# Two MLPs by seven products each level: another order of the first seven products, and operand sums made in halves

## The chip, the cores and the metric

The kernel runs on one core of a Trainium2 chip as one program. The metric is the device time of a run in microseconds. The engines have their own instruction queues and run each queue in order: PE (TensorE, the matrix products), DVE (VectorE), ACT (ScalarE), POOL (GpSimd), and SP, which here only issues DMAs. Engines wait for each other through semaphores.

## The reference, cut to what matters

Two decoder layers over 1024 positions of width 1024, all in float32. Each layer is an attention mixer followed by an MLP, both between norms:

```
x = x + rms_norm(mixer(rms_norm(x)))
x = x + rms_norm(square(relu(rms_norm(x) @ w1)) @ w2)      # w1: 1024x4096, w2: 4096x1024
```

Only the MLP line is touched by the change, in both layers.

## The kernel before, in words

**Products.** The class `Mlp` (L1052) cuts the 4096 inner columns into four groups of 1024. For each group it forms "up", a 1024x1024x1024 product of a weight block with the activations, takes the squared relu, and forms "down", the product with the block of w2, which is added into `acc`. Each such product is not done as eight products of 512x512x512 blocks but as seven, with sums and differences of blocks as operands (a Winograd scheme). The seven have the numbers 1 to 7; `left` (L1101) makes the weight operand and `right` (L1150) the activation operand of a number. In the first group of "up" they are, with weight blocks w00, w01, w10, w11 and activation blocks x00, x10 (first 512 positions) and x01, x11 (last 512):

```
1: w00 * x00          2: w01 * x10          6: s2 * t2        5: (w00 + s2) * (x01 - x00)
7: (w00 - w10) * t3   3: (w01 - s2) * x11   4: w11 * (x10 - t2)
with s2 = w11 - (w00 - w10),  t3 = x11 - x01,  t2 = t3 + x00
```

x11 is the fourth activation block, the one that is complete last; product 3 takes it as it is, unsummed. The sums are written in place where they can be: w01 is overwritten by w01 - s2.

**Precision.** `parts` (L1078) turns every operand of 128x2048 into a rounded part `hi` (ACT, L1083) and a remainder `lo` (L1084, on POOL for weights, on DVE for first-group activations), both in two halves of 1024 columns. One number then is 48 matmuls (L1262): four output quarters j, four inner blocks q, and hi*hi, hi*lo, lo*hi for each. A row names them as out<-moving,stationary.

**Banks.** `product` (L1243) puts the output quarters of a number into one of two sets of PSUM banks by the parity of its place: set A (three `psM` and one `psO`, 512 columns each) or set B (two `psS` pairs of 1024 columns). Numbers 1, 2 and 5 start a sum in their set and the others are accumulated onto what stands there. `evac` (L1268) brings the running sums out: a plain copy by ACT (L1291) when a quarter of the result is first written, and otherwise a DVE addition (L1293) followed by the squared relu (L1294). The old order is 1, 2, 6, 5, 7, 3, 4, with the sets A B A B A B A.

**Order.** `run` (L1313) goes through all 56 steps: `prep` of the next step (operands), `loads` (L1222: DMAs of weights, and, in the first group, stores of the activation operands to DRAM from which later groups read them back), `product`, `evac`. At step 0 it also calls `finish`, which transposes the last 128 positions into x01 and x11 (L369 on PE, copies on ACT L372). This is the order of priority: a scheduler then orders each engine's queue by it and by its own model of when operands are there. Only SP keeps the written order. `Mem` hands out SBUF pages in the order in which they were freed, so an operand can also wait for the last reader of its page.

The sums of operands are all made by one helper, `comb` (L1089), in one DVE instruction of 128x2048 (L1090).

Of the kernel before, what the change touches and what calls it, by code (L numbers as in the profile page):

```python
# [17 lines left out]
ALU = mybir.AluOpType  # L18
# [114 lines left out]
def hybrid_kernel(ctx: ExitStack, tc: tile.TileContext, x, pos, g_mix_pre, g_mix_post, g_ffn_pre, g_ffn_post,  # L133
# [918 lines left out]
    class Mlp:  # L1052
# [5 lines left out]
        UP, DOWN = (1, 2, 6, 5, 7, 3, 4), (1, 5, 6, 3, 7, 2, 4)  # L1058

        def __init__(self, layer):  # L1060
            self.layer = layer
            self.td = tc.dram_tile([7, P, 4096], F32, name=f"t_d{layer}")
            self.w1, self.w2, self.h, self.sums = {}, {}, {}, {}
            self.ready = {}
            self.tq = {}
            self.acc = [None] * 4
            self.steps = []
            for g in range(GROUPS):
                self.steps += [("up", g, n, i) for i, n in enumerate(self.UP)]
                self.steps += [("down", g, n, i) for i, n in enumerate(self.DOWN)]  # L1070
            self.bank = {}
# [17 lines left out]
        def comb(self, out, a, b, op, eng=None):  # L1089
            (eng or nc.vector).tensor_tensor(out, a, b, op=op)  # L1090
            return out
# [9 lines left out]
        def left(self, kind, g, n):  # L1101
# [5 lines left out]
            add, sub = ALU.add, ALU.subtract  # L1107
            if kind == "up":
# [41 lines left out]
        def right(self, kind, g, n):  # L1150
# [4 lines left out]
            if kind == "up":  # L1155
# [6 lines left out]
                elif n == 6:  # L1162
# [3 lines left out]
                    self.comb(t2, t3, r[0, 0], add)  # L1166
                    res = self.parts(t2, lo, True)
# [4 lines left out]
                elif n == 7:  # L1172
                    res = self.parts(r.pop("t3"), lo)
                elif n == 3:
                    res = self.parts(r.pop((1, 1)), lo)
                else:
                    self.comb(r["t2"], r[1, 0], r["t2"], sub)
                    free(r.pop((1, 0)))
                    res = self.parts(r.pop("t2"), lo)
# [63 lines left out]
        def product(self, s, js=range(4)):  # L1243
            kind, g, n, i = self.steps[s]
            (sh, sl), (th, tl) = self.ready[s]
            new = n == 1 or n == (2 if kind == "up" else 5) or n == (5 if kind == "up" else 2)
            if new and js[0] == 0:
                if s % 2:
                    b = [psS(), psS()]
                    self.bank[1] = [b[j // 2][:, j % 2 * 512:(j % 2 + 1) * 512] for j in range(4)], b  # L1250
                else:
                    self.bank[0] = [psM(), psM(), psM(), psO()], None
            bank = self.bank[s % 2][0]
# [14 lines left out]
        def evac(self, s, js=None):  # L1268

            kind, g, n, i = self.steps[s]  # L1270
            banks, pairs = self.bank[s % 2]
# [6 lines left out]
            if kind == "up":  # L1278
                new = {1: (0, 0), 6: (0, 1), 5: (1, 1), 4: (1, 0)}.get(n)
# [465 lines left out]
```

## Time and profile before

| | us |
|---|---|
| median of 3 runs | 2595.79 |
| the runs | 2594.87, 2595.79, 2601.82 |
| profiled execution | 2592.54 |
| its span, first to last instruction | 2590.7 |

Busy in the span: PE 95%, DVE 69%, POOL 52%, ACT 48%. The first MLP's products begin at 750.5 us and the second's at 1947.3 us (one of the second's, in `psO`, is queued as early as 1935.3). A timeline row gives start, duration, engine, line, output<-inputs, shapes, and in brackets how long the engine had been idle before it and what released it. A row with x2 or more is several instructions in a row, with the time from the first's start to the last's end. The granted clock of PE is given as a share of full speed (1.00 is 2.4 GHz, 0.50 is 1.2 GHz).

### The profile page before, as it was taken

The page shows a single profiled execution, that of the slowest core. Times are in us where ns is not written, and L with a number is a line of the kernel's source. Part 1 is how long each engine was busy: PE and PEld are TensorE (multiplying, and loading weights), DVE is VectorE, ACT ScalarE, POOL GpSimd, SP SyncE. Part 2 cuts the span into 40 slices and gives each one's busy share as a digit, 9 for nine tenths or more (in the row PEclk, how much of TensorE's full clock was granted, in tenths as well). Part 3 has the DMA queues.
Part 4 walks back from the last instruction along what each step waited for, and adds up shares of the span by engine and source line. Part 5 has one row for each costly group of instructions (what it writes and reads, how often), then busy time and mean ns, then how long its engine had stood idle before and what let it go on. Part 6 is the DMA issues. An engine that isn't in the chain of part 4 may idle for free.

```text
span 2590.7 us, 33730 instructions
## 1 busy us (share of the span) xinstructions
PE 2461.2 (95%) x12760; PEld 2075.7 (80%) x12760; DVE 1793.7 (69%) x2562; ACT 1254.7 (48%) x2223; POOL 1354.6 (52%) x983
## 2 busy tenths in 40 slices
PE   7999999898998999999999999999998999999997
PEld 6887789776876888888888987777786888888885
DVE  5667999588467629467385568888758946738386
ACT  5554454388443533233235557778744433324233
POOL 4673144666035847667484434333316676757566
PEclk9999999899998999999999999999999999999999
DMA  3011120002435261534504341101235353452613
GB/s 119 17 42 49 47 76 26 1 1 95 137 142 227 101 240 46 206 122 166 192 22 144 142 168 50 50 25 51 92 127 198 127 227 131 163 195 77 240 41 138
DMA packets 74498, 288.97 MB, mean 112 GB/s; under 512 B 6672, under 2 KB 30736, under 8 KB 51808
## 3 DMA queue, kind: packets, MB, share of 16 engines
q1 hardware_dynamic: 67536, 262.63, 27.9%
q0 software_dynamic: 6656, 23.93, 2.5%
q8 instruction: 100, 1.64, 0.3%
q14 instruction: 62, 0.51, 0.1%
q10 hardware_dynamic: 144, 0.26, 0.0%
HBM read 227.03 MB, written 59.77 MB: 111 GB/s over the span
## 4 chain that ended last, share of the span: by engine, by line
PE 73%; DVE 13%; ACT 6%; POOL 3%; issue 2%; DMA 2%; SPq 0%; POOLq 0%; DVEq 0%; ACTq 0%
PE psS L1262 22%; PE psM L1262 17%; PE psO L1262 6%; PE psS L269 3%; PE psS L267 3%; PE psS L268 3%; DVE mask L699 3%; PE psM L925 2%; PE psM L267 2%; PE psM L268 2%; PE psM L269 2%; DVE mask L696 2%; PE psO L913 2%; PE psO L912 1%; PE psS L1630 1%
## 5 line engine op out<-in xcount | busy, mean ns | idle before, releaser
L1084 POOL TENSOR_TENSOR lo<-raw,hi 128x1024 fp32r<-128x1024 f32 x208 | 595.7, 2888 | 265.9 <-ACT hi L1083 203.6
L1083 ACT ACTIVATE hi<-raw 128x1024 fp32r<-128x1024 f32 x208 | 207.9, 1052 | 350.8 <-PE psS L1262 220.8
L901 POOL TENSOR_SCALAR pr<-pr,tot 128x256 f32<-128x256 f32 (+7 forms) x188 | 139.2, 748 | 215.0 <-DVE tot L900 171.0
L1262 PE MATMUL psS<-hi,hi 128*128 128x512 f32 x608 | 239.4, 394 | 8.7 <-DVE acc L1307 3.7
L1262 PE MATMUL psS<-hi,lo 128*128 128x512 f32 x608 | 237.9, 391 | 2.5 <-POOL lo L1084 2.5
L1262 PE MATMUL psS<-lo,hi 128*128 128x512 f32 x608 | 238.0, 391 | 0.0
L1084 POOL TENSOR_TENSOR lo<-s,hi 128x1024 fp32r<-128x1024 f32 x40 | 122.2, 3064 | 162.1 <-ACT hi L1083 87.6
L267 PE MATMUL psM<-wh,hn 128*128 128x256 f32 x576 | 158.1, 291 | 10.0 <-ACT tok L673 5.7
L1083 ACT ACTIVATE hi<-s 128x1024 fp32r<-128x1024 f32 x64 | 64.4, 1054 | 201.0 <-DVE s L1090 201.0
L1262 PE MATMUL psM<-hi,hi 128*128 128x512 f32 x384 | 151.4, 396 | 6.8 <-ACT hi L1083 6.8
L269 PE MATMUL psM<-wh,hn 128*128 128x256 f32 x576 | 155.4, 287 | 0.0
L1262 PE MATMUL psM<-lo,hi 128*128 128x512 f32 x384 | 151.4, 394 | 2.9 <-DVE lo L1084 2.9
L899 ACT ACTIVATE pr<-pr,nm 128x256 f32<-128x256 f32 (+7 forms) x188 | 143.6, 765 | 19.1 <-DVE pr L895 10.9
L268 PE MATMUL psM<-wl,hn 128*128 128x256 f32 x552 | 149.3, 287 | 1.8 <-POOL wl L261 1.8
L1262 PE MATMUL psM<-hi,lo 128*128 128x512 f32 x384 | 151.0, 393 | 0.0
L925 PE MATMUL psM<-idf,pr 128*128 128x128 f32 x834 | 136.6, 277 | 8.8 <-DVE pt L261 4.7
L1262 PEld LDWEIGHTS psS<-hi,hi 128*128 128x128 f32 x608 | 115.2, 189 | 35.5 <-DVE acc L1307 4.5
L1262 PEld LDWEIGHTS psS<-hi,lo 128*128 128x128 f32 x608 | 115.0, 189 | 26.8 <-POOL lo L1084 2.7
L1262 PEld LDWEIGHTS psS<-lo,hi 128*128 128x128 f32 x608 | 114.8, 189 | 23.8
L1090 DVE TENSOR_TENSOR raw<-raw,raw 128x2048 f32<-128x2048 f32 x40 | 105.2, 2633 | 28.5 <-DMA raw<-in_w 28.5
L1293 DVE TENSOR_TENSOR h<-psS,h 128x1024 f32<-128x1024 f32 x32 | 39.1, 1221 | 122.6 <-PE psS L1262 122.6
L267 PEld LDWEIGHTS psM<-wh,hn 128*128 128x128 f32 x576 | 109.4, 196 | 12.6 <-ACT tok L673 7.2
(711 smaller groups left out, 7584.1 us busy)
## 6 DMA issues: line engine op xcount, KB each, us to landing
raw<-in_w SPq DMA_DIRECT2D x64, 1024.0 KB, 7.3
th<-t_d SPq DMA_DIRECT2D x42, 1024.0 KB, 5.0
tl<-t_d SPq DMA_DIRECT2D x42, 1024.0 KB, 7.1
t_d<-hi SPq DMA_DIRECT2D x14, 1024.0 KB, 10.0
t_d<-lo SPq DMA_DIRECT2D x14, 1024.0 KB, 9.5
xt<-xs_d SPq DMA_DIRECT2D x17, 512.0 KB, 4.1
q_d<-qstage POOLq DMA_DIRECT2D x32, 224.0 KB, 3.0
qtok<-q_d SPq DMA_DIRECT2D x8, 896.0 KB, 5.0
```

What stands on the lines that cost most here:

```text
L267: nc.tensor.matmul(dst, lh, rh, start=start, stop=False)
L268: nc.tensor.matmul(dst, lh, rl, start=False, stop=False)
L269: nc.tensor.matmul(dst, ll, rh, start=False, stop=stop)
L696: nc.vector.tensor_scalar(g, sc_, thr_of(j), None, op0=op)
L699: nc.vector.tensor_scalar(box["ge"][:, :nk], sc_, thr_of(j), None, op0=op, op1=ALU.add, accum_out=cnt[:, j:j + 1])
L899: nc.scalar.activation(pt_, pt_, AF.Exp, bias=nm, scale=-1.0, accum_out=tot)
L901: nc.gpsimd.tensor_scalar(pt_, pt_, tot, 1.0, op0=ALU.mult, op1=ALU.mult)
L925: nc.tensor.transpose(m[:, i * P:(i + 1) * P], u["p"][4 * g + i0 + i][:, kb * P:(kb + 1) * P], idf)
L1083: nc.scalar.activation(hi[:, c], v[:, c], AF.Copy)
L1084: eng.tensor_tensor(lo[:, c], v[:, c], f(hi[:, c]), op=ALU.subtract)
L1090: (eng or nc.vector).tensor_tensor(out, a, b, op=op)
L1262: nc.tensor.matmul(bank[j], l[:, a], r[:, b], start=new and q == 0 and m == 0, stop=q == 3 and m == 2, skip_group_check=True)
```

## The change

Three things. In the first group of "up" the order becomes 1, 2, 3, 6, 5, 7, 4, with the bank sets written out beside it: A B B A B A A, so that 2 and 3 stand in set B one after the other, and 7 and 4 in set A. With it, `left` makes s2 and w01 - s2 one step earlier, `right` keeps x11 for t3, and `evac` writes the second quarter of the result from 3 alone by an ACT copy, adds the sum of 1 and 6 to it (four DVE additions of 512 columns, new) and then that of 5, with the squared relu. The other three groups and all "down" products keep their order and their sets. Last, `comb` makes every sum, in all groups, in two instructions of 1024 columns instead of one of 2048.

```diff
@@ -1055,7 +1055,8 @@
-        UP, DOWN = (1, 2, 6, 5, 7, 3, 4), (1, 5, 6, 3, 7, 2, 4)
+        UP, DOWN = ((1, 2, 6, 5, 7, 3, 4), "ABABABA"), ((1, 5, 6, 3, 7, 2, 4), "BABABAB")
+        UP_FIRST = (1, 2, 3, 6, 5, 7, 4), "ABBABAA"
         def __init__(self, layer):
             self.layer = layer
@@ -1064,10 +1065,11 @@
             self.ready = {}
             self.tq = {}
             self.acc = [None] * 4
-            self.steps = []
+            self.steps, self.sets = [], ""
             for g in range(GROUPS):
-                self.steps += [("up", g, n, i) for i, n in enumerate(self.UP)]
-                self.steps += [("down", g, n, i) for i, n in enumerate(self.DOWN)]
+                for kind, (order, sets) in (("up", self.UP if g else self.UP_FIRST), ("down", self.DOWN)):
+                    self.steps += [(kind, g, n, i) for i, n in enumerate(order)]
+                    self.sets += sets
             self.bank = {}
@@ -1087,7 +1089,8 @@
             return hi, lo
         def comb(self, out, a, b, op, eng=None):
-            (eng or nc.vector).tensor_tensor(out, a, b, op=op)
+            for c in (slice(0, 1024), slice(1024, 2048)):
+                (eng or nc.vector).tensor_tensor(out[:, c], a[:, c], b[:, c], op=op)
             return out
         def flat(self, t):
@@ -1105,6 +1108,21 @@
             else:
                 r, lo = self.h, (nc.vector, nc.gpsimd)
             add, sub = ALU.add, ALU.subtract
+            if kind == "up" and g == 0 and n in (2, 3, 6, 5):
+                if n == 2:
+                    res = self.parts(r[0, 1], lo, True)
+                    self.comb(r[1, 0], r[0, 0], r[1, 0], sub)
+                    return res
+                if n == 3:
+                    s2 = r["s2"] = mem([P, 2048], F32, "s2")
+                    self.comb(s2, r[1, 1], r[1, 0], sub)
+                    self.comb(r[0, 1], r[0, 1], s2, sub)
+                    return self.parts(r.pop((0, 1)), lo)
+                if n == 6:
+                    return self.parts(r["s2"], lo, True)
+                self.comb(r[0, 0], r["s2"], r[0, 0], add)
+                free(r.pop("s2"))
+                return self.parts(r.pop((0, 0)), lo)
             if kind == "up":
                 if n == 1:
                     return self.parts(r[0, 0], lo, True)
@@ -1164,6 +1182,7 @@
                     t2 = r["t2"] = mem([P, 2048], F32, "t2")
                     self.comb(t3, r[1, 1], r[0, 1], sub)
                     self.comb(t2, t3, r[0, 0], add)
+                    free(r.pop((1, 1)))
                     res = self.parts(t2, lo, True)
                 elif n == 5:
                     self.comb(r[0, 1], r[0, 1], r[0, 0], sub)
@@ -1172,7 +1191,7 @@
                 elif n == 7:
                     res = self.parts(r.pop("t3"), lo)
                 elif n == 3:
-                    res = self.parts(r.pop((1, 1)), lo)
+                    res = self.parts(r[1, 1], lo, True)
                 else:
                     self.comb(r["t2"], r[1, 0], r["t2"], sub)
                     free(r.pop((1, 0)))
@@ -1243,14 +1262,14 @@
         def product(self, s, js=range(4)):
             kind, g, n, i = self.steps[s]
             (sh, sl), (th, tl) = self.ready[s]
-            new = n == 1 or n == (2 if kind == "up" else 5) or n == (5 if kind == "up" else 2)
+            new = n in (1, 2, 5) or self.steps[s][:3] == ("up", 0, 3)
             if new and js[0] == 0:
-                if s % 2:
+                if self.sets[s] == "B":
                     b = [psS(), psS()]
-                    self.bank[1] = [b[j // 2][:, j % 2 * 512:(j % 2 + 1) * 512] for j in range(4)], b
+                    self.bank["B"] = [b[j // 2][:, j % 2 * 512:(j % 2 + 1) * 512] for j in range(4)], b
                 else:
-                    self.bank[0] = [psM(), psM(), psM(), psO()], None
-            bank = self.bank[s % 2][0]
+                    self.bank["A"] = [psM(), psM(), psM(), psO()], None
+            bank = self.bank[self.sets[s]][0]
             for j in js:
                 for q in range(4):
                     if kind == "up":
@@ -1268,7 +1287,7 @@
         def evac(self, s, js=None):
             kind, g, n, i = self.steps[s]
-            banks, pairs = self.bank[s % 2]
+            banks, pairs = self.bank[self.sets[s]]
             units = [(slice(j, j + 1), banks[j].rearrange("p (a b) -> p a b", b=512)) for j in range(4)]
             if pairs and js is None:
                 units = [(slice(2 * u, 2 * u + 2), pairs[u].rearrange("p (a b) -> p a b", b=512)) for u in range(2)]
@@ -1276,7 +1295,16 @@
                 units = [units[j] for j in js]
             v = nc.vector
             if kind == "up":
-                new = {1: (0, 0), 6: (0, 1), 5: (1, 1), 4: (1, 0)}.get(n)
+                if g == 0 and n in (6, 5):
+                    t = self.hc[0, 1]
+                    for sl_, b in units:
+                        v.tensor_tensor(t[:, sl_], b, t[:, sl_], op=ALU.add)
+                        if n == 5:
+                            v.scalar_tensor_tensor(t[:, sl_], t[:, sl_], 0.0, t[:, sl_], op0=ALU.max, op1=ALU.mult)
+                    if n == 6:
+                        return
+                    self.h[1, 0] = self.flatten(t)
+                new = {1: (0, 0), 5: (1, 1), 4: (1, 0), 6 if g else 3: (0, 1)}.get(n)
                 if new:
                     self.hc = getattr(self, "hc", {})
                     self.hc[new] = mem([P, 4, 512], F32, "h")
```

## Rows read from the trace of the kernel before

**Rows 1.** The page: busy time by engine; chain that ended last, by engine.
```profile
PE 2461.2 (95%) x12760; PEld 2075.7 (80%) x12760; DVE 1793.7 (69%) x2562; ACT 1254.7 (48%) x2223; POOL 1354.6 (52%) x983
...
PE 73%; DVE 13%; ACT 6%; POOL 3%; issue 2%; DMA 2%; SPq 0%; POOLq 0%; DVEq 0%; ACTq 0%
```

**Rows 2.** Stretches: length; busy (instructions) of PE, PEld, DVE, ACT, POOL; PEclk; DMA.
```profile
778.60:792.40 13.80, 3.71 (x7) 1.74 (x6) 13.80 (x8) 9.60 (x10) 7.15 (x2) 0.67 0.18 76
792.40:797.00 4.60, 4.53 (x11) 3.56 (x12) 4.60 (x6) 0.00 (x0) 0.00 (x0) 0.50 0.36 146
797.00:827.00 30.00, 30.00 (x134) 24.83 (x133) 16.34 (x10) 13.97 (x17) 20.73 (x7) 1.00 1.02 398
827.00:1359.00 532.00, 532.00 (x2349) 440.66 (x2348) 335.18 (x208) 184.06 (x207) 348.62 (x124) 1.00 0.36 135
...
1959.00:1978.90 19.90, 14.03 (x57) 10.79 (x56) 14.86 (x4) 3.95 (x6) 18.70 (x6) 0.91 0.26 109
1978.90:1984.30 5.40, 2.57 (x6) 1.16 (x5) 5.40 (x5) 4.17 (x5) 0.00 (x0) 0.73 0.30 121
1984.30:1988.40 4.10, 4.02 (x10) 3.25 (x11) 4.10 (x5) 4.10 (x5) 1.34 (x1) 0.52 0.79 322
1988.40:2030.00 41.60, 41.60 (x185) 34.42 (x184) 41.53 (x18) 17.23 (x20) 34.51 (x11) 1.00 0.82 307
```

**Rows 3.** The chain in order of time, one product of the second MLP.
```profile
2018.00 10.88 PE psS L1262 x48
```

**Rows 4.** Timeline of PE, third product of the first MLP.
```profile
783.41 1.65 PE L1262 MATMUL psM<-hi,hi 128*128 128x512 f32 x3 [4.77 <-ACT hi L1083]
...
789.07 0.80 PE L1262 MATMUL psS<-hi,hi 128*128 128x512 f32 x1 [2.51 <-DVE h L1293]
792.47 0.79 PE L1262 MATMUL psM<-lo,hi 128*128 128x512 f32 x1 [2.61 <-DVE lo L1084]
```

**Rows 5.** Timeline of DVE, first MLP.
```profile
749.77 1.22 DVE L325 TENSOR_TENSOR xn<-xn,xt 128x1024 f32<-128x1024 f32 x1
...
768.02 4.45 DVE L1090 TENSOR_TENSOR raw<-raw,s 128x2048 f32<-128x2048 f32 x1 [5.11 <-POOL lo L1084]
772.88 3.99 DVE L1090 TENSOR_TENSOR t<-xb,xb 128x2048 f32<-128x2048 f32 x1 [0.41 <-ACT xb L372]
...
777.93 2.28 DVE L1090 TENSOR_TENSOR t<-t,xb 128x2048 f32<-128x2048 f32 x1
...
787.80 1.21 DVE L1293 TENSOR_TENSOR h<-psS,h 128x1024 f32<-128x1024 f32 x1
...
819.63 3.41 DVE L1084 TENSOR_TENSOR lo<-h,hi 128x1024 fp32r<-128x1024 f32 x1
822.97 0.68 DVE L1293 TENSOR_TENSOR h<-psM,h 128x512 f32<-128x512 f32 x1
```

**Rows 6.** Timeline of ACT: the last piece of x11, first MLP.
```profile
772.25 0.60 ACT L372 ACTIVATE xb<-psS 128x512 f32<-128x512 f32 x1 [6.48 <-PE psS L369]
```

**Rows 7.** Timeline of POOL, first and second MLP.
```profile
763.31 11.41 POOL L1084 TENSOR_TENSOR lo<-raw,hi 128x1024 fp32r<-128x1024 f32 x4 [2.57 <-ACT h L1291]
...
1957.55 6.72 POOL L1084 TENSOR_TENSOR lo<-s,hi 128x1024 fp32r<-128x1024 f32 x2 [4.96 <-ACT hi L1083]
1964.24 13.46 POOL L1084 TENSOR_TENSOR lo<-raw,hi 128x1024 fp32r<-128x1024 f32 x4
```

**Rows 8.** Timeline of PE, second and third product of the second MLP.
```profile
1962.20 0.63 PE L369 MATMUL psS<-idf,xn 128*128 128x128 f32 x4 [3.17 <-DVE xn L312]
...
1966.63 0.50 PE L1262 MATMUL psS<-hi,lo 128*128 128x512 f32 x1 [2.47 <-POOL lo L1084]
...
1984.38 0.80 PE L1262 MATMUL psM<-lo,hi 128*128 128x512 f32 x1 [0.28 <-DVE lo L1084]
```

**Rows 9.** Timeline of DVE, second MLP: evacuation of number 7.
```profile
2018.87 0.68 DVE L1293 TENSOR_TENSOR h<-psM,h 128x512 f32<-128x512 f32 x1
...
2030.21 0.68 DVE L1293 TENSOR_TENSOR h<-psO,h 128x512 f32<-128x512 f32 x1
```

## Prediction

> **What bounds the kernel now.** I read the page first: PE is busy 95% of the span and holds 73% of the chain that ended last [rows 1]. Then I laid windows over both MLPs. From 827 to 1359 PE is busy for 532.00 of 532.00 us at clock 1.00 while DVE works 335.18 and POOL 348.62 [rows 2]: there nothing that DVE does can gain or lose time as long as it keeps up. The chain in order of time gives the price of a product: 10.88 us for 48 matmuls, 0.227 us each [rows 3]. The change can earn only where PE stands or runs slow, and in the MLPs that is their first group.
>
> In the first MLP the hole is the third product, number 6: from 778.6 to 797.0 PE runs 7 and 11 matmuls, the 11 at granted clock 0.50, the 1.2 GHz level, after it had idled [rows 2]. 18 matmuls are worth 4.1 us, so 18.4 - 4.1 = 14.3 us are lost. The timeline of PE names who ended each wait: ACT's hi, a DVE addition that frees a `psS` pair, DVE's lo [rows 4]. Behind all three stands DVE, busy for 13.80 of the 13.80 us [rows 2]. x11 is complete at 772.85 [rows 6]; then t3 runs for 3.99 us and t2 after it before anything of number 6 can be rounded [rows 5]. In the second MLP the same place is 1978.9 to 1988.4: 9.5 us with 16 matmuls, worth 3.6, so 5.9 us lost, the later part again at clock 0.52 [rows 2]. Together 20.2 us.
>
> The second product loses time too. In the second MLP it waits 3.17 us for the norm's DVE step and 2.47 us for the lo of w01 on POOL [rows 8].
>
> **The change part by part.** The profiled execution took 2592.54 us, of which 2590.7 is its span; the median shown is 2595.79, 3.25 above it. I sum against 2592.54 and add the 3.25 at the end.
>
> *Number 3 third.* It needs x11 rounded and w01 - s2, and neither t3 nor t2. x11 ends at 772.85; two ACT halves and two DVE halves of 1.22 us [rows 5] fit before the second product ends at 778.6. w01 - s2 may be written only when POOL has read w01: in the trace the sum starts at 768.02, after a 5.11 us wait for that lo [rows 5]. Its rounding on POOL costs two halves of 11.41 / 4 = 2.85 us [rows 7], one behind the other, and the second is due only at the third product's half, 5.4 us in. So number 3 can start as the second product ends. That takes 14.3 and 5.9 us out: **-20.2**.
>
> *What is late next.* Number 6 is now due at 778.6 + 10.9 = 789.5. From 772.85 DVE must make two halves each of lo x11, t3, t2 and lo t2, and two pair additions of 1.21 us [rows 5]: 8 x 1.22 + 2.4 = 12.2 us, if nothing disturbs it. But a DVE half takes 3.41 us where POOL is busy and 1.22 where it is not [rows 5]: 2.2 us more, about one POOL turn. The extra goes by how many POOL halves fall into the stretch: at least the two of w01 - s2, at most six with those of s2 and of w00 + s2. So 12.2 + 4.4 = 16.6 to 12.2 + 13.2 = 25.4 us, ready at 789.5 to 798.3, a wait of 0 to 8.8. I take four turns, since POOL ran four halves in a row from 763.31 [rows 7]: 793.9, a wait of 4.4, less the hi*hi matmuls that can go ahead, some 4 x 0.227 us. A short wait may also drop the clock again for some ten matmuls, as in the 4.60 us with 11 matmuls [rows 2]. **+4** in the first MLP.
>
> In the second MLP, DVE is the tight one: busy in 5.40 of 5.40, 4.10 of 4.10 and 41.53 of 41.60 us up to 2030 [rows 2], against 16.34 of 30.00 in the same part of the first. There POOL works 18.70 of 19.90 us before 1978.9 [rows 2], so six turns: two halves more, those of w01 - s2, give 14.6 + 13.2 = 27.8 us from 1964.8 (POOL's second run begins at 1964.24 [rows 7] as x11 comes complete), ready at 1992.6 against 1978.9 + 10.9 = 1989.8. That is 2.8 us. To it comes the new work: the addition of number 6, 4 x 0.68 = 2.7 us [rows 5], on an engine with no idle time. Bounds: 0, if the scheduler puts the relu steps behind, to the whole 5.9. **+4.5**.
>
> *Same banks twice.* Number 3 overwrites set B as soon as number 2 is out of it, and number 4 adds onto set A right behind 7. Pair one is done when the product is half through and its addition takes 1.21 us; pair two must be out 24 matmuls, 5.4 us, after the product's end. The cover is gone that a product in the other set gave. In the trace the second pair's addition started at 787.80 [rows 5], 9.2 us after the end. With number 3 instead of number 6 behind it, the additions come first in priority, and halves let them in sooner; I take them as in time, **0**, and keep 0 to 5 us per MLP for the range. For 7 and 4 the second MLP's rows are near the limit: product 7 ended at 2018.0 [rows 3], its last bank was added at 2030.89 [rows 9], 12.9 us later, where number 4 would need it 36 matmuls, 8.2 us, after the start. That is 4.7 us if the lag stays; in the first MLP the first addition came at 822.97 [rows 5], before the product's end. Part of it is in the +4.5.
>
> *Halves elsewhere.* Two halves cost 2 x 1.22 instead of 2.28, 0.16 us more [rows 5], and up to one more turn of 2.2 (a whole sum beside POOL took 4.45, one turn over 2.28 [rows 5]). A later product brings one sum on the average and two at most (the listing of `left` and `right`), so up to 2.4 to 4.7 us in 10.88; DVE idles 37% of 827 to 1359 [rows 2], 4.0 us per product. PE hides it: **0**; if that cover failed, it would be 0.7 us on a product with two sums, some ten products per MLP.
>
> *Second product.* s2's rounding, which stood on POOL ahead of w01's in the second MLP (1957.55 before 1964.24 [rows 7]), now has the lower priority, and sums in halves hold up the norm's DVE step less. Between 0 and 5.6 us [rows 8]; both orders hang on when pages come free, so I take **-1**. The stores of number 3's activations stand on SP two places earlier and all later ones behind them; SP only waits there for operands that PE needs sooner anyway.
>
> Sum: -20.2 + 4 + 4.5 - 1 = -12.7 us, 2579.8 on the profiled run's scale, **2583** on the median's.
>
> **The rivals.**
>
> *DVE keeps pace.* If DVE fills the gaps of POOL (it idles 13.7 of the 30 us from 797 [rows 2]) and in the second MLP w01 is rounded first, only some 2 us of the waits stay: -20.2 + 2 - 3 = -21, 2575. For it: the 13.7 us. Against it: DVE has no idle us in the second MLP.
>
> *The hole only moves.* POOL and DVE take turns in nearly every half, so number 6 comes late by almost what number 3 gained. With eight turns in the first MLP: 12.2 + 17.6 = 29.8 us, ready at 802.7, 13 us late; in the second the gain of 5.9 goes whole. -20.2 + 13 + 5.9 = -1, 2594; with five to seven turns up to -7. For it speaks that every DVE half beside POOL in the trace costs a turn (3.41 against 1.22 [rows 5]), so that one sum of 4.45 us becomes two halves of 3.4, 6.8 together. Against it: POOL had only two halves in the 13.8 us of the old hole [rows 2]. The Trainium skill (SBUF — State Buffer, "Who interferes with whom") states it as a rule: a DVE instruction with two SBUF inputs and a GpSimd one that reads SBUF exclude each other for the whole instruction, so smaller DVE instructions give POOL more openings. By that rule the halves speak against this change; the trace agrees with one turn per instruction, and whether a turn is lost for each of the new halves no row shows.
>
> *The banks decide, slower.* The second pair of number 2 comes out as late as at 787.80: 9.2 + 1.2 - 5.4 = 5.0 us of wait, then about 2 us at half clock as in the 11 matmuls; and 4 waits for 7's banks, 4.7 us and again 2. That is 14 us per MLP, 28 in all against 20.2 earned: +8, 2604. It decides from 20 us on, that is where both waits occur in both MLPs. For it: rows 9. Against it: the first MLP's 822.97, and that the scheduler knows the bank's dependence.
>
> *The order isn't taken up.* The scheduler may place t3 and t2 on DVE ahead of x11's lo. As x11's hi takes one ACT half, t3 can slip in, and number 3 is late by 2 to 4 us; that lies inside the forecast's range.
>
> **How the numbers follow.** About 0.3%, 7.8 us, is what a measurement here can tell from no change: 2588 to 2603.6. Forecast (8 to 17 us gained) 0.47; DVE keeps pace 0.19; the hole moves 0.24, of which I count all as within the bound; banks 0.10, mostly slower by more. So faster 0.66, same 0.25, slower 0.09. The likeliest case alone spans 2579 to 2588. The range goes from 2570, where the second product's 5.6 us and all of the hole come in, to 2599, which takes in the moved hole and half of the bank case.
>
> **What would show it.** Right: PE without a gap from number 2 into 3, DVE's lo of x11 before 778 and 1978; a gap of 2 to 5 us before number 6, ended by DVE's lo; number 4 behind 7 with under 3 us of waiting, on L1293. The steady stretches stay at 10.88 us per product. Wrong: a wait on L1293 of 5 us or more before the second half of number 3; a gap before 6 as long as the old one; gaps in the later groups, where halves would then be too dear; or a changed time before 750, which no step of mine touches.

## The result, and the profile after

The changed kernel takes 2617.06 us (median of 4 runs, 2610.71 to 2618.18) against 2596.15 for the kernel before beside it (2594.87 to 2601.82): ratio 1.0078, 95% interval [1.006, 1.0095]. It is slower by 0.8%; forecast were 2583 us and a range up to 2599. Its profiled execution took 2616.35 us with a span of 2614.6, 23.9 more than before.

The page of the changed kernel, busy time by engine and the chain that ended last by engine:

```profile
PE 2463.7 (94%) x12760; PEld 2075.7 (79%) x12760; DVE 1839.9 (70%) x2674; ACT 1257.4 (48%) x2219; POOL 1327.5 (51%) x983
...
PE 59%; DVE 21%; ACT 6%; POOL 5%; issue 5%; DMA 2%; SPq 0%; POOLq 0%; DVEq 0%; ACTq 0%
```

Against [rows 1], PE has the same work, and DVE holds 21% of the chain in place of 13%: somewhere PE now waits for DVE. From the start of the first matmul of an MLP's products to that of the last, PE's timeline gives 631.2 and 640.3 us before, 639.2 and 654.5 after: 8.0 us more in the first MLP, 14.3 in the second. The rest of the difference is that the first MLP begins 1.1 us later, and 0.4 us between the two.

Windows over the changed kernel (columns as in rows 2): the third to sixth product of the first MLP; the place where number 4 follows 7 on the same banks; the rest of that MLP; number 3 behind 2 in the second MLP, and 4 behind 7 there:

```profile
777.00:829.50 52.50, 51.03 (x224) 41.46 (x222) 47.98 (x29) 24.63 (x25) 39.30 (x13) 1.00 0.71 260
829.50:846.00 16.50, 7.01 (x19) 5.54 (x19) 16.40 (x16) 2.68 (x3) 3.24 (x1) 0.69 0.00 0
860.00:1386.00 526.00, 522.64 (x2298) 430.56 (x2298) 336.60 (x244) 180.49 (x205) 329.62 (x124) 1.00 0.38 141
1982.40:1999.00 16.60, 5.93 (x15) 4.18 (x15) 16.60 (x11) 8.85 (x9) 8.48 (x4) 0.59 0.31 127
2039.70:2050.50 10.80, 4.22 (x12) 3.33 (x12) 10.80 (x12) 1.02 (x1) 0.35 (x1) 0.68 0.00 1
```

The old hole of the first MLP, 7 and 11 matmuls in 18.4 us at clock 0.67 and 0.50 [rows 2], is gone: 224 matmuls in 52.50 us at clock 1.00, nearly the 0.227 us each of [rows 3]. In its place stand the second, fourth and fifth line. In each of the three DVE is busy for practically the whole stretch and PE runs 12 to 19 matmuls at a mean clock of 0.59 to 0.69. The third line isn't whole either: 3.4 us without PE, where [rows 2] had none.

PE's timeline of the changed kernel, the matmuls that began with a wait (in brackets its length, and who ended it):

```profile
771.38 0.79 PE L1281 MATMUL psS<-hi,lo 128*128 128x512 f32 x1 [3.80 <-POOL lo L1086]
...
839.02 0.80 PE L1281 MATMUL psM<-hi,hi 128*128 128x512 f32 x1 [9.48 <-DVE h L1321]
...
1028.05 0.47 PE L1281 MATMUL psS<-hi,hi 128*128 128x512 f32 x1 [1.00 <-DVE acc L1335]
...
1988.44 1.65 PE L1281 MATMUL psM<-hi,hi 128*128 128x512 f32 x3 [5.99 <-ACT hi L1085]
1995.19 0.80 PE L1281 MATMUL psS<-hi,hi 128*128 128x512 f32 x1 [4.68 <-DVE h L1321]
...
2046.33 0.80 PE L1281 MATMUL psM<-hi,hi 128*128 128x512 f32 x1 [6.58 <-DVE h L1321]
```

L1321 is the addition that empties a bank. Number 4 stands 9.48 us in the first MLP and 6.58 in the second until 7 is added out of its first bank. In the second MLP PE has the first 4 matmuls of number 6 (`psM`) in its queue ahead of number 3 (`psS`): it stands 5.99 us for their operand, t2 rounded by ACT, and then 4.68 us until 2's first pair is out, which ends last. In the first MLP, 16 matmuls of number 6 fill the time before number 3 from 784.2 on, and only the second pair costs a wait, 1.47 us at 795.06. The first matmuls after the long waits take 0.79 or 0.80 us, as those in [rows 4], in the stretch that [rows 2] has at clock 0.50. From one start of a matmul to the next, less 0.227 us each, 12.6 us are lost at 839, 13.8 from 1982.4 on and 8.5 at 2046. The wait of 1.00 us on L1335 comes three times in each MLP, once in each later group, and each loses 1.24 us, at clock 1.00 throughout.

What DVE did meanwhile, from its timeline in the changed kernel (start, length, with `x2` both halves together):

```profile
820.44 6.75 DVE L1093 TENSOR_TENSOR raw<-raw,raw 128x1024 f32<-128x1024 f32 x2
827.11 1.21 DVE L1301 TENSOR_TENSOR h<-psS,h 128x1024 f32<-128x1024 f32 x1
828.25 5.58 DVE L1093 TENSOR_TENSOR raw<-raw,raw 128x1024 f32<-128x1024 f32 x2
...
834.88 1.21 DVE L1093 TENSOR_TENSOR raw<-raw,raw 128x1024 f32<-128x1024 f32 x1
...
837.15 1.21 DVE L1093 TENSOR_TENSOR raw<-raw,raw 128x1024 f32<-128x1024 f32 x1
838.28 0.68 DVE L1321 TENSOR_TENSOR h<-psM,h 128x512 f32<-128x512 f32 x1
...
1026.69 1.21 DVE L1335 TENSOR_TENSOR acc<-psS,acc 128x1024 f32<-128x1024 f32 x1
...
1980.60 3.40 DVE L1093 TENSOR_TENSOR raw<-raw,s 128x1024 f32<-128x1024 f32 x1
1983.93 3.37 DVE L1093 TENSOR_TENSOR t<-t,xb 128x1024 f32<-128x1024 f32 x1
1987.22 3.38 DVE L1093 TENSOR_TENSOR xb<-xb,xb 128x1024 f32<-128x1024 f32 x1
...
1993.92 1.21 DVE L1321 TENSOR_TENSOR h<-psS,h 128x1024 f32<-128x1024 f32 x1
```

Ahead of the addition that PE waits for stand operand sums. In the first MLP, from 820.44, they are those of the second weights, for products after number 4, which nothing needs yet; three of these six halves take 3.4 us in place of 1.21. In the second MLP they are nearer to their use: the half of w01 - s2 at 1980.60 is for number 3 itself, t2 at 1983.93 is the operand for which PE stands until 1988.44, and only x01 - x00 at 1987.22 could have come later. Before, 7 ran from 815.11 on PE and its first addition came at 822.97 [rows 5]; now 7 runs from 818.49 and the addition comes at 838.28. POOL's timeline of the changed kernel shows the second product's wait:

```profile
763.37 4.68 POOL L1086 TENSOR_TENSOR lo<-s,hi 128x1024 fp32r<-128x1024 f32 x2 [3.87 <-PE psO L1281]
768.01 6.64 POOL L1086 TENSOR_TENSOR lo<-raw,hi 128x1024 fp32r<-128x1024 f32 x2
```

POOL rounds s2, the operand of the fourth product, and only then w01, that of the second.

### The profile page after: what moved, and what is told of

Its sections match the earlier page's. It is cut to its first block, busy times and chain, and to the rows that moved or that the text cites. A ratio compares the mean times of both kernels' runs of the same rounds, so it can differ in the third digit from the quotient of the medians.

```text
span 2614.6 us, 33860 instructions
## 1 busy us (share of the span) xinstructions
PE 2463.7 (94%) x12760; PEld 2075.7 (79%) x12760; DVE 1839.9 (70%) x2674; ACT 1257.4 (48%) x2219; POOL 1327.5 (51%) x983
## 4 chain that ended last, share of the span: by engine, by line
PE 59%; DVE 21%; ACT 6%; POOL 5%; issue 5%; DMA 2%; SPq 0%; POOLq 0%; DVEq 0%; ACTq 0%
PE psS L1281 15%; PE psM L1281 13%; PE psO L1281 4%; DVE raw L1093 3%; PE psS L269 3%; PE psS L267 3%; PE psS L268 3%; DVE mask L699 3%; PE psM L925 2%; POOL lo L1086 2%; PE psM L267 2%; PE psM L268 2%; PE psM L269 2%; DVE lo L1086 2%; DVE s L1093 2%
## 5 line engine op out<-in xcount | busy, mean ns | idle before, releaser
L1086 POOL TENSOR_TENSOR lo<-raw,hi 128x1024 fp32r<-128x1024 f32 x208 | 576.1, 2792 | 299.0 <-ACT hi L1085 248.7
L1086 POOL TENSOR_TENSOR lo<-s,hi 128x1024 fp32r<-128x1024 f32 x40 | 115.2, 2888 | 158.4 <-PE psS L1281 56.4
L1093 DVE TENSOR_TENSOR raw<-raw,raw 128x1024 f32<-128x1024 f32 x80 | 149.9, 1888 | 26.6 <-DMA raw<-in_w 26.3
L925 PEld LDWEIGHTS psM<-idf,pr 128*128 128x128 f32 x834 | 97.8, 141 | 28.7 <-DVE pt L261 8.9
L267 PEld LDWEIGHTS psM<-wh,hn 128*128 128x128 f32 x576 | 109.4, 196 | 12.6 <-ACT tok L673 7.2
```

The lines of the kernel that those rows point to most:

```text
L267: nc.tensor.matmul(dst, lh, rh, start=start, stop=False)
L925: nc.tensor.transpose(m[:, i * P:(i + 1) * P], u["p"][4 * g + i0 + i][:, kb * P:(kb + 1) * P], idf)
L1086: eng.tensor_tensor(lo[:, c], v[:, c], f(hi[:, c]), op=ALU.subtract)
L1093: (eng or nc.vector).tensor_tensor(out[:, c], a[:, c], b[:, c], op=op)
```

## The experiments

The first group's order is 1, 2, 3, 6, 5, 7, 4, and `parts` writes the rounded half (`hi`, ACT) and the remainder (`lo`, DVE or POOL) of an operand. Medians are beside a kernel before of 2594.3 to 2596.3 us in each lot.

| run | what it is | median us | ratio to before, 95% |
|---|---|---|---|
| e1 | new order, whole sums | 2612.42 | 1.0069 [1.0053, 1.0085] |
| e2 | old order, sums in halves | 2600.50 | 1.0025 [1.0015, 1.0034] |
| f4 | old order, halves in the first group's up alone | 2593.06 | 0.9998 [0.9986, 1.0009] |
| e3 | changed kernel, additions first on DVE | 2603.18 | 1.0030 [1.0020, 1.0041] |
| e4 | e1, additions first | 2592.69 | 0.9991 [0.9981, 1.0000] |
| f1 | changed kernel, w01 first on POOL | 2609.50 | 1.0066 [1.0047, 1.0085] |
| f2 | e4, w01 first on POOL | 2591.76 | 0.9991 [0.9980, 1.0001] |
| f3 | f2, number 2's relu later | 2592.53 | 0.9995 [0.9984, 1.0005] |
| g3 | e4 without three relus | 2583.45 | 0.9958 [0.9944, 0.9972] |
| g4 | before without three relus | 2594.66 | 0.9997 [0.9988, 1.0007] |
| g1 | e4, first up remainders on DVE | 2575.27 | 0.9927 [0.9914, 0.9940] |
| g2 | before, the same remainders on DVE | 2595.03 | 1.0000 [0.9989, 1.0010] |
| h1 | changed kernel, the same | 2581.19 | 0.9952 [0.9938, 0.9965] |
| h2 | e1, the same | 2575.99 | 0.9932 [0.9918, 0.9947] |

**The two parts of the change, apart.** e1 is the changed kernel with the sums whole:

```diff
-            for c in (slice(0, 1024), slice(1024, 2048)):
-                (eng or nc.vector).tensor_tensor(out[:, c], a[:, c], b[:, c], op=op)
+            (eng or nc.vector).tensor_tensor(out, a, b, op=op)
```

> The new order and sets, the sums whole again as before. Theory (two separate costs: DVE additions that free a bank set stand behind operand sums in DVE's queue, 21 us in the two first groups; halves cost about 8 us in the later groups, 1.24 us at each group's start): the 8 us go and the waits before number 4 stay in part, so 2601 to 2611 us, slower than before by 5 to 15; no wait of PE on acc in the later groups. Rival A (the halves are the whole loss, since DVE is slowed everywhere): at or below before, 2575 to 2597. Rival B (the order is the whole loss): 2613 to 2619, as the changed kernel.

e2 is the kernel before with that edit the other way round.

> The old order and sets, the sums in halves. Theory: the later groups lose 1.24 us at three group starts per MLP and the first groups change by a few us either way: 2600 to 2607 us, 4 to 11 above before. Rival A (halves are the whole loss): 2612 to 2622. Rival B (order is the whole loss): 2593 to 2599.

e1 took 2612.42, just past its theory's range and 0.6 us short of its rival B's, e2 2600.50, within its theory's. The order alone costs 17.8 us and the halves alone 5.9 (both against 2594.59); together that is 23.7, somewhat more than the change's 20.9, and the order is the greater part. In e1 the bank waits are there without any half; PE's timeline of e1:

```profile
772.82 0.80 PE L1280 MATMUL psS<-hi,lo 128*128 128x512 f32 x1 [4.92 <-POOL lo L1086]
...
840.28 0.79 PE L1280 MATMUL psM<-hi,hi 128*128 128x512 f32 x1 [10.49 <-DVE h L1320]
...
2045.41 0.80 PE L1280 MATMUL psM<-hi,hi 128*128 128x512 f32 x1 [5.61 <-DVE h L1320]
```

In e2 it is DVE's timeline that shows the price of a half, at the third down product of a later group, which adds onto the bank set of the first. The accumulation L1308, which frees that pair, comes at 1020.92, behind the first half of a weight sum, and PE starts 1.01 us late at 1022.28:

```profile
1018.65 1.21 DVE L1091 TENSOR_TENSOR s<-h,s 128x1024 f32<-128x1024 f32 x1
1019.78 1.21 DVE L1091 TENSOR_TENSOR raw<-raw,raw 128x1024 f32<-128x1024 f32 x1
1020.92 1.21 DVE L1308 TENSOR_TENSOR acc<-psS,acc 128x1024 f32<-128x1024 f32 x1
```

In the kernel before the accumulation came ahead of that sum:

```profile
1016.24 1.21 DVE L1307 TENSOR_TENSOR acc<-psS,acc 128x1024 f32<-128x1024 f32 x1
1017.37 3.36 DVE L1090 TENSOR_TENSOR raw<-raw,raw 128x2048 f32<-128x2048 f32 x1
```

f4 is the control, halves only in the first group's up (`prep` notes the group; the lines between are left out):

```diff
-            (eng or nc.vector).tensor_tensor(out, a, b, op=op)
+            for c in (slice(0, 1024), slice(1024, 2048)) if self.first else (slice(0, 2048),):
+                (eng or nc.vector).tensor_tensor(out[:, c], a[:, c], b[:, c], op=op)
...
+            self.first = g == 0 and kind == "up"
```

> The kernel before with its order and bank sets, and operand sums in halves in the first group's up products alone. Theory: the 5.9 us that halves cost with the old order lie in the later groups, where each last down product's addition stands behind halves (six turns of 1.25 us); without them 2592 to 2597 us, no change. Rival, the halves cost where DVE has most sums, in the first group of each MLP: 2598 to 2602 us.

2593.06: no cost there. So the halves' 5.9 us lie elsewhere; e2's trace has the wait of 1.0 us at six places, all in the later groups.

**Queue orders.** e3 puts on DVE all that `prep` issues for the products 6 and 5 behind number 2's first and second addition, and what it issues for the down products 5, 6 and 3 behind number 7's last; e4 does the same to e1:

```diff
-                        v.tensor_tensor(d, b, d, op=ALU.add)
+                        self.adds[s, sl_.start // (sl_.stop - sl_.start)] = v.tensor_tensor(d, b, d, op=ALU.add).ins
...
-                self.prep(s + 1)
+                behind = {3: (1, 0), 4: (1, 1), 8: (5, 3), 9: (5, 3), 10: (5, 3)}.get(s + 1)
+                with tc.issue_after(self.adds[behind]) if behind else ExitStack():
+                    self.prep(s + 1)
```

> The changed kernel, but in the first group DVE's operand sums and remainders of number 6 are queued behind the first pair's addition of number 2, those of number 5 behind the second pair's, and the three next steps of down behind the last addition of number 7. Nothing else is changed. Theory: the waits of PE on the additions (9.5 and 1.5 us in the first MLP, 6.6 and 4.7 in the second) fall under 2 us each, with the half clock behind them, so some 20 us less: 2592 to 2602 us. Rival A (halves): DVE is as slow as before, only the names of the waits change: 2610 to 2620.

> The new order with whole sums, and the additions queued first as in e3. Theory: both costs gone, what the order gained until the sixth product (7 us) and more of it is left: 2578 to 2592 us, 4 to 18 below before. Rival A: as e1, at or below before. Rival B (the order itself costs): above 2605.

e3 gives back 14 us and e4 20; both times end about 1 us above the range of their theory. The late additions are a matter of DVE's queue, then. One wait of the second MLP stays in e3: with the bank free early, PE still stands 5.10 us at 1987.07 for the operand of number 6, whose first matmuls it has ahead of number 3. And e4, with them cured and no halves, is only level with the kernel before. Its PE waits are on POOL's remainders (w01's, 3.91 us, in the first MLP, and those of w01 - s2, 4.43, at number 3 in the second) and on DVE's remainders for number 6 (1.11 and 2.29, 1.13 and 3.61). f1 and f2 turn POOL's order (cut; `self.w01_lo` is the last remainder of w01 - s2):

```diff
...
                 if n == 6:
-                    return self.parts(r["s2"], lo, True)
+                    with tc.issue_after(self.w01_lo):
+                        return self.parts(r["s2"], lo, True)
```

> The changed kernel with one order on POOL's queue turned: the remainders of s2 (the operand of the sixth product by number, fourth in order) stand behind those of w01 - s2 (the third product's) and so behind w01's (the second product's). Theory: the second product of the first MLP waits 3.8 us for POOL's remainder only because s2's stand ahead of it, and the third of the second MLP for the like reason; without that 5 to 9 us go: 2607 to 2612 us. Rival A, the place in POOL's queue is not what holds the second product (the sums ahead of the remainder on DVE are): 2614 to 2618 us. Rival B, the time comes back as a wait of the fourth product (number 6) for s2's remainders, now later: 2614 to 2620 us, with that wait 4 us or more in the trace.

> New order of the products with whole sums, with the operand sums and remainders on DVE queued behind the additions that set the banks free, and with POOL's s2 remainders behind those of w01 - s2. Theory (four prices add up: two in DVE's queue, one in POOL's, one in the halves): the two waits left on POOL's remainders, 6.6 us in the first MLP and 4.4 in the second, go down to about 2 and 1: 2583 to 2588 us, faster than the kernel before by 0.2 to 0.5 percent. Rival, number 6 waits instead for s2's remainders or for DVE's remainder of t2: 2590 to 2594 us, no faster than the same kernel without POOL's order (2592.7).

f1, 2609.5, is within its theory's range, but not for the theory's reason. In the first MLP the wait of 3.80 us goes, and then PE stands for number 6's operand and for the bank of number 3:

```profile
778.95 1.65 PE L1284 MATMUL psM<-hi,hi 128*128 128x512 f32 x3 [3.35 <-ACT hi L1085]
...
786.17 0.80 PE L1284 MATMUL psS<-hi,hi 128*128 128x512 f32 x1 [5.14 <-DVE h L1324]
```

Up to 850 that MLP loses 22.9 us in place of the changed kernel's 23.3, counted as above. What f1 gains lies in the second MLP, where number 4 waits 2.30 us in place of 6.58. f2 is outside its theory: 2591.76, the rival's result. The wait on POOL went and came back at number 6 and at number 4, as PE's timeline of f2 shows:

```profile
770.58 0.50 PE L1284 MATMUL psS<-hi,lo 128*128 128x512 f32 x1 [0.34 <-POOL lo L1087]
...
800.53 0.76 PE L1284 MATMUL psM<-lo,hi 128*128 128x512 f32 x1 [4.38 <-DVE lo L1087]
...
836.97 0.50 PE L1284 MATMUL psM<-hi,hi 128*128 128x512 f32 x1 [2.27 <-DVE h L1324]
```

f3 takes what stood ahead of that remainder out of the way, number 2's squared relu:

```diff
                         self.adds[...] = v.tensor_tensor(d, b, d, op=ALU.add).ins
+                        if s == 1:
+                            self.relus.append(d)
+                            continue
...
+                if s == 3:
+                    with tc.issue_after(self.last_lo):
+                        for d in self.relus:
+                            nc.vector.scalar_tensor_tensor(d, d, 0.0, d, op0=ALU.max, op1=ALU.mult)
```

> The kernel of the run with whole sums and both queue orders, and besides the squared relu of product number 2 on DVE behind the remainders that products 6 and 5 need. Theory: what number 6 still waits for (two waits of 1.4 and 4 to 6.5 us in each MLP, on DVE's remainder of t2) is that squared relu ahead of it in DVE's queue, 4 pieces of about 2.3 us; with it later 4 to 10 us go in all: 2575 to 2583 us. Rival, the relu only moves in front of the next thing that is late (number 5's remainders or the addition of number 7): within 2 us of the run without it, 2583 to 2590.

2592.53: the rival again, within 1 us of f2, though above the range that it gave. In the first MLP number 6 waits 2.67 us at 796.13 in place of 4.38, and number 4 waits 4.76 at 835.76 in place of 2.27. Three orders of the queues (e4, f2, f3) end within 1 us of each other. That would fit a queue that is full, in which only what stands last changes; the next two runs test it.

**Is DVE full, and of what?** g3 leaves the squared relus of 2, 5 and 7 out of e4's first group, g4 those of 2, 3 and 7 out of the kernel before (the lines are g4's; in g3 that of 5 goes from the new order's own lines too):

```diff
                         v.tensor_tensor(d, b, d, op=ALU.add)
-                        v.scalar_tensor_tensor(d, d, 0.0, d, op0=ALU.max, op1=ALU.mult)
+                        if g:
+                            v.scalar_tensor_tensor(d, d, 0.0, d, op0=ALU.max, op1=ALU.mult)
```

> New order, whole sums, additions first, and the squared relu on DVE of products 2, 5 and 7 left out in the first group (part of the computation is not done). Theory (DVE is the bound there): number 2's two pieces of 3.42 us stand ahead of the remainders of t2 that number 6 waits for, so nearly all of that wait, 5.5 us and 7.9 us, goes: 8 to 14 us less, 2579 to 2585 us. Rival, DVE's queue is not the bound, number 6 waits for the chain from the loads over the sums: 2589 to 2593 us.

> The kernel before with the squared relus on DVE of products 2, 3 and 7 left out in the first group (part of the computation is not done). Theory: in the old order the third product waits for DVE work that stands beside or behind number 2's addition, and the squared relu of number 2 is ahead of part of it: 0 to 8 us less, 2588 to 2596 us, less than in the new order. Rival, DVE bounds the old order as tightly as the new: 8 to 14 us less, 2582 to 2588 us.

Both as expected: the new order gains 9.2 us from less DVE work (2592.69 to 2583.45), the old one nothing measurable. With the new order DVE is the bound of the first group. With the old one it isn't: in g4 number 6 still waits 4.77 us for ACT to round t2, as in [rows 4], which points to the chain through t3 and t2. DVE's timeline of f2 shows what it is full of:

```profile
797.10 3.38 DVE L1087 TENSOR_TENSOR lo<-t,hi 128x1024 fp32r<-128x1024 f32 x1
800.40 3.40 DVE L1325 SCALAR_TENSOR_TENSOR h<-h 128x1024 f32<-128x1024 f32 x1
803.73 3.42 DVE L1087 TENSOR_TENSOR lo<-t,hi 128x1024 fp32r<-128x1024 f32 x1
807.07 6.75 DVE L1087 TENSOR_TENSOR lo<-xb,hi 128x1024 fp32r<-128x1024 f32 x2
```

Five pieces at 3.4 us each, which take 1.22 where POOL rests. In e4, POOL's pieces take 3.41 in the mean on the weight tiles, and 2.34 each at 763.00, where DVE waits for ACT. 3.4 is about 1.2 + 2.2, as if the two engines went in turn, one piece each. So a piece on DVE and one on POOL together take 3.4 us, while DVE alone makes two in 2.44. What is given to POOL there to relieve DVE makes DVE later.

g1, g2, h1 and h2 make the test. One line puts the remainders of the first group's up weight operands, 14 pieces in each MLP, from POOL on DVE, in e4 (g1), the kernel before (g2), the changed kernel as it is (h1) and e1 (h2):

```diff
             if kind == "up":
-                r, lo = self.w1, (nc.gpsimd, nc.gpsimd)
+                r, lo = self.w1, (nc.gpsimd, nc.gpsimd) if g else (nc.vector, nc.vector)
```

> New order, whole sums, additions first (the kernel that took 2592.7 us), and the remainders of the first group's up weight operands, 14 pieces of 128x1024 in each MLP, on DVE in place of POOL. Theory (DVE is the bound of the first seven products because each of its pieces beside a POOL piece takes 3.4 us in place of 1.22): 14 pieces of 1.22 come to DVE, 17 us, and the stretching of some 15 others, 2.2 us each, goes, 33 us; the waits of the fourth product, 5.5 us and 7.9 us, and those on POOL, 6.6 and 6.0 us, shrink by a half or more: 2578 to 2587 us. Rival, DVE is full by its own work and each piece more makes it later: 2594 to 2612 us.

> The kernel before with the same edit, 14 remainders of each MLP's first up group on DVE in place of POOL. Theory: in the old order DVE's remainders are not stretched (1.22 to 1.6 us each in that stretch), so there is less to win back, while 17 us of work come to DVE: 2589 to 2600 us, no gain over 0.3 percent. Rival, POOL's work beside DVE's costs the old order as much as the new: 2578 to 2588 us.

> The changed kernel as it is (order, bank sets, halves, DVE's queue) with the remainders of the first group's up weight operands on DVE in place of POOL. Theory that the stretching makes the additions late: the 9.5 and 6.6 us that number 4 waits for number 7's additions shrink by a half or more and the waits on POOL's remainders go: 2590 to 2602 us. Rival, the queue's order makes them late whatever a piece takes, and the second weights' remainders, still on POOL, stretch the sums ahead of the additions as before: only the waits on POOL's remainders go, 2603 to 2613 us.

> The new order alone with whole sums (2612.4 us) and the same remainders on DVE, without the additions put first. Theory that the stretching makes the additions late: 2582 to 2595 us, near the run that has the additions first as well (2575.3). Rival, the queue's order by itself: number 4 still waits 5 us or more behind number 7 in each MLP, 2598 to 2608 us.

g1: 2575.27, 17.4 us below e4 and 2.7 below its theory's range. g2: nothing. h1: 2581.19, 35.9 below the changed kernel (34.0 when each is taken against the kernel before beside it) and below its theory's range; the change as made, with that line, is faster than the kernel before by 0.48%. h2: 2575.99, below its theory's range too and the same as g1, though nothing puts the additions first there; number 4 waits 1.73 and 1.76 us in it, in e1 10.49 and 5.61. So the additions need not be forced ahead when POOL's remainders are out of the way. That doesn't show that the stretched pieces alone made the banks late, as the scheduler's order on DVE changed with the edit. In the changed kernel all six half sums of the second weights stand ahead of 7's first addition; in h1 four of them follow it:

```profile
819.33 0.68 DVE L1321 TENSOR_TENSOR h<-psM,h 128x512 f32<-128x512 f32 x1
819.93 4.62 DVE L1093 TENSOR_TENSOR raw<-raw,raw 128x1024 f32<-128x1024 f32 x4
```

Only from e4 to g1, with the additions held first in both, does the move act with that order fixed: 17.4 us. Groups of the same stretch, 765 to 850, by line, operation and shape (count, busy time, mean ns of one); first the changed kernel:

```profile
L1093 DVE TENSOR_TENSOR raw<-raw,raw 128x1024 f32<-128x1024 f32 x6 | 14.7, 2483 | 0.0
...
L1086 DVE TENSOR_TENSOR lo<-xb,hi 128x1024 fp32r<-128x1024 f32 x4 | 10.2, 2566 | 0.0
...
L1086 POOL TENSOR_TENSOR lo<-raw,hi 128x1024 fp32r<-128x1024 f32 x14 | 45.9, 3301 | 15.6 <-ACT hi L1085 15.6
```

and h1:

```profile
L1086 DVE TENSOR_TENSOR lo<-raw,hi 128x1024 fp32r<-128x1024 f32 x8 | 13.3, 1672 | 0.0
...
L1093 DVE TENSOR_TENSOR raw<-raw,raw 128x1024 f32<-128x1024 f32 x7 | 8.2, 1212 | 0.0
...
L1086 DVE TENSOR_TENSOR lo<-xb,hi 128x1024 fp32r<-128x1024 f32 x4 | 4.8, 1223 | 0.0
...
L1086 POOL TENSOR_TENSOR lo<-raw,hi 128x1024 fp32r<-128x1024 f32 x6 | 17.7, 2968 | 47.9 <-DVE lo L1086 41.2 <-ACT hi L1085 6.7
```

The eight weight remainders that came to DVE in that stretch cost it 13.3 us; the sums fell from 2.48 to 1.21 us each and the remainders of the `xb` tiles (x11 among them) from 2.57 to 1.22. Windows of h1, to be laid beside the first two of the changed kernel:

```profile
777.00:829.50 52.50, 51.69 (x227) 42.14 (x226) 52.50 (x46) 20.67 (x21) 14.82 (x5) 1.00 0.61 240
829.50:846.00 16.50, 16.50 (x75) 13.66 (x74) 16.43 (x11) 9.46 (x11) 12.68 (x4) 1.00 0.00 1
```

DVE is busier than in the changed kernel (52.50 of 52.50 in place of 47.98) and has 46 instructions done where it had 29; PE is whole from 829.50 on, where number 4, begun at 820.06, is nearly done. A busy share doesn't tell work from waiting for a turn. PE's timeline of h1 has the first MLP's wait of number 4 down to 0.49 us, and the longest wait left in the second MLP is one for an operand:

```profile
820.06 0.50 PE L1281 MATMUL psM<-hi,hi 128*128 128x512 f32 x1 [0.49 <-DVE h L1321]
...
1965.94 1.65 PE L1281 MATMUL psM<-hi,hi 128*128 128x512 f32 x3 [3.26 <-ACT hi L1085]
```

The 5.2 us from h1 to h2 fit the halves of the later groups: h1 has the three waits of 1.00 us in the first MLP's, h2 none. g1 and h2 are the fastest of all: 0.73% and 0.68% below the kernel before. Not told apart is which counts more, DVE's pieces made longer or POOL's remainders made late: g1's edit removes both.

## Why the prediction was wrong

The step that failed is "I take them as in time, 0": the additions that free a bank set used twice in a row came late. PE's timelines give the whole account of the 22.3 us that the two MLPs lost, in round terms: -20.2 for the old holes, +1.7 left of the first, +34.9 where a bank set is used twice, +7.4 for the halves in the later groups, -1.5 at the second product.

- **Number 3 third, -20.2: right in the first MLP.** The loss from 778.6 to 797.0 is gone but for 1.47 us. The scheduler has PE begin number 6 between 2 and 3, which the rival "the order isn't taken up" put down to DVE. g4 agrees that the old hole wasn't DVE's amount of work. The second MLP's 5.9 us were exchanged for 13.8. Number 3 couldn't have run through there even with its bank free: DVE's remainder of x11, which the text wanted before 1978, ended at 1991.73.
- **What is late next, +4 and +4.5: too much in the first MLP**, where number 6 began at 784.2 without a wait. In the second, number 6's operand was late by 5.99 us, inside the time that the bank took anyway; in e3, where the bank is free early, 5.10 us of it stay.
- **Same banks twice, 0: wrong, and the largest error.** Measured are 12.6, 13.8 and 8.5 us, 35 in all; of the 13.8 half, 6.9 us, had gone on number 6's operand before the wait for the bank began. The text took the additions as in time because "the additions come first in priority". In fact operand sums stood ahead of them, in the first MLP those of products after number 4; e3 and e4, which turn only that order, give back 14 and 20 us. The rival "the banks decide" had the mechanism and its sites, with a chance of 0.10, and 28 us for the two MLPs; of its four waits the one in the first MLP at set B hardly came (1.47 us), the other three were dearer. Number 4's waits of 9.48 and 6.58 us are past the 3 us that the text set as a sign.
- **Halves elsewhere, 0: wrong by 6**, the gaps in the later groups that the text named as a sign. The text counted how much DVE work PE can hide and found cover; the cost isn't in the amount. A sum cut in two leaves DVE free at another moment, a half slips in ahead of the accumulation that frees a bank, and PE waits 1.00 us and loses 1.24, three times in each MLP. e2 and f4 show it.
- **Second product, -1: -1.5 measured, by luck.** Until number 2 ends, the first MLP loses 8.9 us in place of 4.3, the second 2.4 in place of 8.5. In the first, s2's remainders went ahead of w01's on POOL, against the text; in the second they went behind, as it said. Turning that order in f1 didn't win the first MLP's loss back.
- **The deeper step is in "what is late next".** The text had the turn of 2.2 us per DVE piece beside POOL from [rows 5], and used it for the readiness of one operand. It did not carry it on to all that DVE has to do until number 4. The third product early brings number 6's, 5's and 7's operands and the second weights' together with POOL's remainders; in the old order the hole kept them apart, and DVE's remainders of the `xb` and `t` tiles took 1.22 and 1.58 us in the mean there, not 2.57 and 2.01 (765 to 850). With the turn taken away, h1 came to 2581.19, near the forecast of 2583, though with the halves' loss in it and work moved from POOL. That is no proof of the other terms; it shows that most of the 34 us between forecast and result hang on POOL's remainders standing beside DVE's work, and leaves open how much of it is stretching, how much the order that the scheduler then makes.
- **"The hole only moves"** (2594) describes e4, f2 and f3: with banks and POOL's order mended, what number 3 gains is lost again at 6 and 4. Its reason, turns with POOL, fits g1. The Trainium skill's rule cited there (SBUF — State Buffer, "Who interferes with whom") agrees with f2's five pieces of 3.4 us, and the trace gives it a price: 2.2 us for a DVE piece of 128x1024.
- A further sentence of the Trainium skill (Perfetto Trace Analysis, "Optimizing Scalar/DVE Operations") says that moving work between VectorE and GpSimd may not help, as they share a read port of SBUF. The runs go further, in one place: in the new order it did harm to have the 14 remainders on POOL (17.4 us by g1, 35.9 by h1), in the old none (g2).

## What to carry to other kernels

Before an order is made tighter, add up for the stretch not only what each engine has to do but what each piece costs when the two engines that take turns are active together; a piece on POOL beside a full DVE cost more DVE time (2.2 us) than making it on DVE would have (1.22). When several orders of a queue give the same time, take work or contention out of the queue and stop turning it. And cutting an instruction of an engine that is off the path isn't free if that engine also frees PE's banks: look at what stands just ahead of each freeing instruction.

## What the hardware showed that was not expected

- The additions out of PSUM were not stretched. L1301 on a `psS` pair took 1.21 us in the changed kernel at 827.11, with POOL at work from 826.06 to 832.74, as long as L1321 at 1993.92, where POOL rests; pieces with both inputs in SBUF took up to 3.42 beside POOL, the squared relu, which reads one SBUF tile as both inputs, among them (3.40 at 800.40 in f2).
- A wait cost more than its length: 9.48 us of waiting lost 12.6 and 6.58 lost 8.5, since the matmuls right after it ran at clock 0.50 (839.00 to 845.00, 2046.30 to 2049.90). After the 1.00 us in the later groups the clock stayed at 1.00, and what it lost beyond its length, 0.24, is mostly a matter of counting: matmuls take 0.39 us and start 0.227 apart, and the wait is counted only from the end of the last one.
